# A two-layer hybrid decoder trunk: the two rstd biases of the first layer computed on VectorE instead of GpSimd

## The chip, the core and the metric

The kernel runs on one core of a Trainium2 chip. Its engines work side by side, each through its own list of instructions in order: TensorE (PE: matmuls; PEld: its weight loads), ScalarE (ACT), VectorE (DVE), GpSimd (POOL) and SyncE (SP), whose queue issues the DMAs here. An instruction waits for semaphores that instructions of other engines, or landing DMAs, raise. The metric is the device time of one execution in microseconds (us). A profile covers one execution, and its span runs from the first to the last instruction of the program.

## What is computed

Two layers work on x of 256 positions by 1024 channels in float32. Each normalises x, projects it, runs three branches of heads on parts of the projection, gates them, projects the result back and adds it to x. A last normalisation follows. The part that matters here is the normalisation of the first layer:

```python
def rms_norm(x, gain):
    xf = x.astype(jnp.float32)
    xf = xf * lax.rsqrt(jnp.mean(xf * xf, axis=-1, keepdims=True) + EPS)
    return (xf * gain.astype(jnp.float32)).astype(x.dtype)

def hybrid_layer(x, ...):
    hn = rms_norm(x, norm_gain)
    proj = jnp.einsum('bsd,de->bse', hn, w_in)
    a_q, a_k, a_v, a_g, b_x, b_g, c_q, c_k, c_v, c_g = jnp.split(proj, ...)
    # branch A: rotary positions, dilated attention
    # branch B: convolution and a gated linear recurrence
    # branch C: stick-breaking attention
    y = jnp.concatenate([y_a, y_b, y_c], axis=-1)
    return x + jnp.einsum('bse,ed->bsd', y, w_out)
```

## The kernel before

The 256 positions are two tiles of 128 partitions (t = 0 and 1), the 1024 channels eight tiles of 128 (k). A float32 product is made of three passes of matmuls over operands split in a high part and a remainder: `xh`, `xl` for the activations, `whi`, `wlo` for the weights. The passes are (whi, xh), (whi, xl), (wlo, xh), in this order (`mm3`, L202 to L207).

The weights come in chunks of 128 x 2048 (`load_chunk`, L95 to L105): for each half, SP issues a DMA of 512 KB into a buffer `st` (L100); ScalarE copies it in two pieces to `whi` (L103), and VectorE subtracts to get `wlo` (L104). There are five `st` buffers (`WST`, L32), and a buffer can be loaded again once the `wlo` pieces made from it are done. The order of the chunks is fixed: the values of branch A and C are made from the `first` loads (L136 to L165), then follow the chunks CQ and CK (queries and keys of branch C), AQ0 and AK0 (queries and keys of the first four heads of A), BX (branch B), AQ1 and further.

In the first layer the projections start from x scaled by the gain only; the factor rstd of each position is put on afterwards. `rms_stats(t)` (L186) makes it: ScalarE squares the two halves of `xres` (x as it was loaded) and sums each along the channels (L189, the sum goes to `sq`); then GpSimd makes `ss` = sq0 / 1024 + EPS (L191), and ScalarE makes `ln` = Ln(sq1 / 1024 + ss), with `ss` as the bias, and rstd = Exp(-0.5 ln) (both through the helper at L82). ScalarE then uses rstd to evict the values (`va`, L318, and `vc`, L319). VectorE uses it at L310: two diagonal matrices, which TensorE multiplies by ones (L311), so that rstd lies along a row; VectorE copies that to `rb` (L312) and scales with it the queries `qc` and keys `kc` of branch C (L324). The scores of branch C (`sb_scores`, L372 to L379) need `qc` and `kc`.

Each engine runs its list in order. TensorE's list is in the order of the code (`tc.manual_schedule`, L90, names PE alone); those of ScalarE, VectorE, GpSimd and SP come from the scheduler of the tile framework. GpSimd has little to do: it computes `log_sigmoid_lambda` (L231 to L254), a chain of some 25 instructions on tiles of 128 x 4, each waiting for the one before, whose results `c8` and `nc8` are used much later in branch B. After that chain, in its list, stand the six instructions of L191: two for the first layer, two for the second, two for the last normalisation.

On ScalarE the first layer's list around the change is: pieces of CQ (L103), the two squares of t = 0, Ln of t = 0, the two squares of t = 1 with Exp of t = 0 between them, `va` and `vc` with Ln and Exp of t = 1 between them, and then the pieces of CK, AQ0, AK0, BX, and the first half of AQ1.

Of the kernel before, what the change touches and what calls it, by code (L numbers as in the profile page):

```python
# [13 lines left out]
ALU = mybir.AluOpType  # L14
# [3 lines left out]
D = 1024  # L18
L = 2
NT = S // P  # L20
# [4 lines left out]
EPS = 1e-6  # L25
# [22 lines left out]
def trunk_kernel(ctx: ExitStack, tc: tile.TileContext, x, first_x, first, wpack, prm_d, gatew, gains, consts, rope, out):  # L48
    nc = tc.nc
    act, dve, pe, gps = nc.scalar, nc.vector, nc.tensor, nc.gpsimd  # L50
# [13 lines left out]
    def scr(w):  # L64
        return wk.tile([P, 512], F32, name="scr", tag="scr", bufs=SCR)[:, 0:w]
# [15 lines left out]
    def tab(*a, **k):  # L81
        i = dep(act.activation(*a, **k), loaded["load"])  # L82
        loaded["users"].append(i)
        return i
# [98 lines left out]
    idb = cst.tile([P, P], BF16, name="idb")  # L183
    cmb = cst.tile([P, P], BF16, name="cmb")

    def rms_stats(t):  # L186
        sq = wk.tile([P, 2], F32, name="sq", tag="sq", bufs=2)
        for i in range(2):
            act.activation(scr(512), xres[:, t, i * 512:(i + 1) * 512], AF.Square, accum_out=sq[:, i:i + 1])  # L189
        ss = wk.tile([P, 1], F32, name="ss", tag="ss", bufs=2)  # L190
        gps.tensor_scalar(ss, sq[:, 0:1], 1.0 / D, EPS, ALU.mult, ALU.add)  # L191
        ln = wk.tile([P, 1], F32, name="lnv", tag="lnv", bufs=2)
        tab(ln, sq[:, 1:2], AF.Ln, bias=ss, scale=1.0 / D)
        rstd = wk.tile([P, 1], F32, name="rstd", tag="rstd", bufs=4)
        tab(rstd, ln, AF.Exp, scale=-0.5)
        return rstd
# [10 lines left out]
            pe.matmul(ps, a(k), b(k), start=first and i == 0, stop=last and i == len(seq) - 1)  # L207

    def normed(t):
        rstd = rms_stats(t)  # L210
        xns = []
        for half in range(2):
            xn = scr(512)
            cs = slice(half * 512, half * 512 + 512)
            dve.scalar_tensor_tensor(xn, xres[:, t, cs], rstd, gn[:, cs], ALU.mult, ALU.mult)
            xns.append(xn)
        return xns
# [43 lines left out]
    for l in range(L):  # L261
# [27 lines left out]
        if l > 0:  # L289
            xn1 = normed(1)  # L290
            av_w = [weights(l, CH_AV + i, 1 - i) for i in range(2)]
            cv_w = weights(l, CH_CV, 0)
            av_ps, cv_ps = [], bank(pp, "pp")
            for t in range(NT):
                av_ps.append(bank(at, "s"))
                for i in range(2):
                    proj_a(av_ps[t], av_w[i], t, 4 * i, 4, 512, i == 0, i == 1)
                if t == 0:
                    turn(xn1, 1, xh, xl)
                proj_a(cv_ps[:, t * 256:(t + 1) * 256], cv_w, t, 0, 8, 256, True, True)  # L300
            cv_bk = [cv_ps[:, t * 256:(t + 1) * 256] for t in range(NT)]

        if l == 0:
            rstd0 = [rms_stats(t) for t in range(NT)]

        def rows_of_rstd():
            rb_ps = bank(yp, "y")
# [270 lines left out]
        for t in range(NT):  # L578
            if t == 1 and l == 0:
                next_x = [sb.tile([P, NK, S], F32R, name=n, tag=n) for n in ("xh", "xl")]  # L580
                xn0 = normed(0)
            for n2 in range(2):
                cs = slice(n2 * 512, n2 * 512 + 512)
                for ks in ((0, 1), (2, 3)):
                    out_mm(o_ps[t, n2], ow[n2], t, 1, ks, False, ks[0] == 2)
                    if (l, t, n2, ks[0]) == (0, 1, 1, 0):
                        turn(xn0, 0, *next_x)
                dve.tensor_add(xres[:, t, cs], o_ps[t, n2], xres[:, t, cs])  # L588

    for t in range(NT):  # L590
        rstd = rms_stats(t)
        for half in range(2):
            cs = slice(half * 512, half * 512 + 512)
            ot = scr(512)
            dve.tensor_mul(ot, xres[:, t, cs], gf[:, cs])
            if half == 0:
                dve.tensor_scalar(ot, ot, rstd, None, ALU.mult)
            else:
                act.activation(ot, ot, AF.Copy, scale=rstd)
            nc.sync.dma_start(out=out[t * P:(t + 1) * P, cs], in_=ot)  # L600
# [108 lines left out]
```

## Time and profile before

| | us |
|---|---|
| median of 3 runs | 257.91 |
| lowest and highest of them | 255.73, 257.99 |
| the profiled execution, whole | 258.01 |
| its span | 256.2 |
| TensorE busy | 245.9 (96% of the span) |
| VectorE busy | 190.8 (74%) |
| ScalarE busy | 163.7 (64%) |
| GpSimd busy | 9.5 (4%) |

Times of a view count from the start of the span. In rows of the timeline stand the start, the length, the engine, the line, the operation, what is written and read with sizes, how many instructions are merged, and in brackets how long the engine had been idle just before and what ended that. A row of the chain of waits has the start, the length and what ran. A row of the view of waits has the waiting instruction, what it waited for, the total, the number of waits and the longest.

### The profile page before, as it was taken

Reading aid. Unit: us, or ns where it says so; the run is one execution under the profiler, and the core shown is the slowest. Engines: PE = TensorE matmul, PEld = TensorE weight load, DVE = VectorE, ACT = ScalarE, POOL = GpSimd, SP = SyncE. Lnnn points to the kernel's source line nnn. Section 1 sums busy time; section 2 is a strip of 40 time slices with the busy share of each in tenths; the row PEclk is TensorE's granted clock in tenths of the full one; section 3 lists DMA queues with packets and bytes.
Section 4 is the critical chain, followed back from the end, with each engine's and each line's share of the span. In section 5 each row is a group of like instructions: output and inputs, shape, how many; then the busy total and the mean of one; then the engine's idle time right before and its main releaser. Section 6 shows DMA issues by size and latency. Waiting matters only on the chain.

```text
span 256.2 us, 4730 instructions
## 1 busy us (share of the span) xinstructions
PE 245.9 (96%) x1777; PEld 223.7 (87%) x1777; DVE 190.8 (74%) x427; ACT 163.7 (64%) x355; POOL 9.5 (4%) x35
## 2 busy tenths in 40 slices
PE   7999699999999999999999999999999999999990
PEld 3889599999899899978889899999999979987870
DVE  4873299999999778996594564499999856894243
ACT  3864967964594669994582765594485468993143
POOL 0037000000000000000010000000000000000000
PEclk9999979999999999999999999999999999999997
DMA  7989679862526815157448387522643742000022
GB/s 224 376 291 409 240 226 314 296 236 82 160 88 216 263 62 164 36 186 278 159 124 258 112 283 276 181 89 77 185 145 115 236 145 79 5 0 0 3 82 82
DMA packets 13126, 43.44 MB, mean 170 GB/s; under 512 B 1584, under 2 KB 2224, under 8 KB 13104
## 3 DMA queue, kind: packets, MB, share of 16 engines
q1 hardware_dynamic: 12816, 42.89, 49.6%
q8 instruction: 14, 0.23, 0.3%
q10 hardware_dynamic: 288, 0.26, 0.3%
q14 instruction: 8, 0.07, 0.1%
HBM read 42.09 MB, written 1.05 MB: 168 GB/s over the span
## 4 chain that ended last, share of the span: by engine, by line
PE 86%; DMA 4%; ACT 3%; POOL 3%; issue 1%; DVE 1%; SPq 0%; ACTq 0%
PE pp L207 63%; PE s L207 9%; DMA st<-first 4%; PE y L358 3%; PE s L426 2%; PE s L455 2%; PE s L399 1%; PE pp L481 1%; POOL ls L249 1%; POOL ls L248 1%; PE s L372 1%; PE s L223 1%; ACT scr L189 1%; ACT whi L153 1%; PE s L379 0%
## 5 line engine op out<-in xcount | busy, mean ns | idle before, releaser
L104 DVE TENSOR_TENSOR wlo<-st,whi 128x512 fp32r<-128x512 f32 x132 | 84.7, 688 | 26.3 <-ACT whi L103 25.7
L103 ACT ACTIVATE whi<-st 128x512 fp32r<-128x512 f32 x132 | 74.1, 623 | 35.8 <-PE pp L207 17.2
L207 PE MATMUL pp<-xh,whi 128*128 128x256 f32 x352 | 51.2, 287 | 2.4 <-ACT whi L103 2.4
L207 PE MATMUL pp<-xl,whi 128*128 128x256 f32 x352 | 50.2, 286 | 0.0
L207 PEld LDWEIGHTS pp<-xh,whi 128*128 128x128 f32 x352 | 46.2, 193 | 4.4 <-ACT whi L103 3.1
L207 PE MATMUL pp<-xh,wlo 128*128 128x256 f32 x352 | 49.6, 284 | 0.0
L207 PEld LDWEIGHTS pp<-xl,whi 128*128 128x128 f32 x352 | 46.2, 195 | 0.0
L207 PEld LDWEIGHTS pp<-xh,wlo 128*128 128x128 f32 x352 | 45.7, 193 | 0.0
L82 ACT ACTIVATE pr<-scr,mn 128x128 f32<-128x128 f32 (+1 forms) x32 | 14.1, 445 | 9.2 <-DVE mn L433 9.2
L189 ACT ACTIVATE scr<-xres 128x512 f32<-128x512 f32 x12 | 7.5, 626 | 13.0 <-DVE xres L588 12.9
L207 PE MATMUL pp<-whi,yh 128*128 128x512 f32 x48 | 14.1, 394 | 0.0
L207 PE MATMUL pp<-wlo,yh 128*128 128x512 f32 x48 | 13.8, 390 | 0.0
L207 PE MATMUL pp<-whi,yl 128*128 128x512 f32 x48 | 13.8, 389 | 0.0
L76 ACT ACT_TABLE_LOAD x9 | 11.5, 1283 | 1.8 <-PEq L702 1.6
L82 ACT ACTIVATE scr<-scr 128x384 f32<-128x384 f32 (+1 forms) x20 | 10.8, 540 | 0.5 <-DVE scr L324 0.3
L207 PEld LDWEIGHTS pp<-wlo,yh 128*128 128x128 f32 x48 | 9.0, 188 | 1.9
L207 PEld LDWEIGHTS pp<-whi,yl 128*128 128x128 f32 x48 | 9.0, 188 | 1.9
L207 PEld LDWEIGHTS pp<-whi,yh 128*128 128x128 f32 x48 | 8.7, 188 | 1.6
L191 POOL TENSOR_SCALAR ss<-sq 128x1 f32<-128x1 f32 x6 | 1.8, 306 | 221.3 <-ACT scr L189 220.2
L346 ACT ACTIVATE yh<-scr 128x512 fp32r<-128x512 f32 x8 | 5.1, 633 | 7.6 <-DVE scr L345 7.5
L433 DVE CUSTOM_DVE_ANT_0 scr<-s,con 128x128 f32<-128x128 f32 (+1 forms) x32 | 9.2, 354 | 0.6 <-PE s L426 0.6
L588 DVE TENSOR_TENSOR xres<-pp,xres 128x512 f32<-128x512 f32 x6 | 4.1, 690 | 7.3 <-PE pp L207 7.3
(160 smaller groups left out, 353.5 us busy)
## 6 DMA issues: line engine op xcount, KB each, us to landing
st<-w_pack SPq DMA_DIRECT2D x66, 512.0 KB, 5.0
st<-first SPq DMA_DIRECT2D x7, 512.0 KB, 5.6
xres<-x_in SPq DMA_DIRECT2D x2, 512.0 KB, 8.2
out<-scr SPq DMA_DIRECT2D x4, 256.0 KB, 2.2
gw_t<-gate_w SPq DMA_DIRECT2D x2, 256.0 KB, 6.5
gn<-gains SPq DMA_DIRECT2D x1, 512.0 KB, 6.5
gf<-gains SPq DMA_DIRECT2D x1, 512.0 KB, 6.0
st<-first ACTq DMA_DIRECT2D x2, 128.0 KB, 3.5
```

Source lines behind the costliest of these rows:

```text
L76: load = act.preload_act_table_set(name)
L82: i = dep(act.activation(*a, **k), loaded["load"])
L103: act.activation(hi[:, ws], st[:, ss], AF.Copy)
L104: dve.tensor_sub(lo[:, ws], st[:, ss], hi[:, ws].bitcast(F32))
L189: act.activation(scr(512), xres[:, t, i * 512:(i + 1) * 512], AF.Square, accum_out=sq[:, i:i + 1])
L207: pe.matmul(ps, a(k), b(k), start=first and i == 0, stop=last and i == len(seq) - 1)
L346: act.activation(yh[:, k0:k0 + n, :], dst, AF.Copy)
L358: pe.matmul(y[hr, p * 128 + o:p * 128 + 256], vt[:, s0, hs], wts[i][:, ws], start=s0 == 0, stop=s0 == 1)
L426: pe.matmul(sps[h][:, cs], qT[h0][hr, hb, t * P:(t + 1) * P], kT[h0][hr, hb, 0:(t + 1) * P], start=True, stop=True)
L433: dve.tensor_tensor_reduce(xs[:, cs], sps[h][:, cs], nmask[:, cs], -0.125, 3e38, ALU.add, ALU.min, mn[:, t:t + 1])
L455: pe.transpose(tp[:, i * P:(i + 1) * P], prob[h0 + h][:, j * P:(j + 1) * P], ident)
L588: dve.tensor_add(xres[:, t, cs], o_ps[t, n2], xres[:, t, cs])
```

## The change

`rms_stats` gets the engine of its bias instruction as an argument. The calls of the first layer hand it VectorE; the calls of the second layer (through `normed`) and of the last normalisation hand it GpSimd, as before. The operation, its operands and its result are the same.

```diff
-    def rms_stats(t):
+    def rms_stats(t, eng):
         sq = wk.tile([P, 2], F32, name="sq", tag="sq", bufs=2)
         for i in range(2):
             act.activation(scr(512), xres[:, t, i * 512:(i + 1) * 512], AF.Square, accum_out=sq[:, i:i + 1])
         ss = wk.tile([P, 1], F32, name="ss", tag="ss", bufs=2)
-        gps.tensor_scalar(ss, sq[:, 0:1], 1.0 / D, EPS, ALU.mult, ALU.add)
+        eng.tensor_scalar(ss, sq[:, 0:1], 1.0 / D, EPS, ALU.mult, ALU.add)
...
-        rstd = rms_stats(t)
+        rstd = rms_stats(t, gps)
...
-            rstd0 = [rms_stats(t) for t in range(NT)]
+            rstd0 = [rms_stats(t, dve) for t in range(NT)]
...
-        rstd = rms_stats(t)
+        rstd = rms_stats(t, gps)
```

In VectorE's list of the first layer, the place is between the last remainders of the chunk CQ and those of the chunk CK (`wlo_381`); the numbers behind names count the tiles as they are made, so `ss_306` is that of t = 0 and `ss_317` that of t = 1:

```order
 L104 TENSOR_TENSOR wlo_268<-st_269,whi_267 128x512 x2
 L104 TENSOR_TENSOR wlo_268<-st_275,whi_267 128x512 x2
+L191 TENSOR_SCALAR ss_306<-sq_301 128x1
+L191 TENSOR_SCALAR ss_317<-sq_312 128x1
 L512 CAST idb_291<-con_284 128x128
 L104 TENSOR_TENSOR wlo_381<-st_382,whi_380 128x512 x2
```

Both instructions now stand ahead of the cast of the identity `idb` and of all work on CK.

In GpSimd's list, the place is the end of the chain of `log_sigmoid_lambda`, whose last two instructions write `c8` and `nc8`:

```order
 L253 TENSOR_SCALAR c8_293<-c8_293 128x4
 L254 TENSOR_SCALAR nc8_294<-c8_293 128x4
-L191 TENSOR_SCALAR ss_306<-sq_301 128x1
-L191 TENSOR_SCALAR ss_317<-sq_312 128x1
 L191 TENSOR_SCALAR ss_1602<-sq_1597 128x1
 L191 TENSOR_SCALAR ss_1659<-sq_1654 128x1
```

They no longer stand behind that chain; the instruction that follows it now belongs to the second layer. The lists of TensorE, ScalarE and SP have the same instructions in the same order as before.

## The prediction, made before the changed kernel had run

> **What bounds the kernel now.** I read the view of waits of TensorE first, since it is busy for 96% of the span: once for the whole span, then for 36 to 250 us, where it has no row at all. Its one wait of size comes before that:
>
> ```profile
> PE pp L207 <- ACT whi L103: 2.4, 1, 2.4
> ```
>
> So the kernel goes at the speed of TensorE from 36 us on, and what can be won from outside it lies ahead of that. The timeline of TensorE shows what stands around this wait:
>
> ```profile
> 26.05 1.12 PE L207 MATMUL pp<-xl,whi 128*128 128x256 f32 x8
> 27.01 1.12 PE L207 MATMUL pp<-xh,wlo 128*128 128x256 f32 x8
> 30.54 2.35 PE L207 MATMUL pp<-xh,whi 128*128 128x256 f32 x8 [2.41 <-ACT whi L103]
> 32.70 1.91 PE L207 MATMUL pp<-xl,whi 128*128 128x256 f32 x8
> 34.40 1.35 PE L207 MATMUL pp<-xh,wlo 128*128 128x256 f32 x8
> 35.59 0.60 PE L311 MATMUL y<-scr,ones 128*128 128x128 f32 x4
> 35.95 1.20 PE L207 MATMUL pp<-xh,whi 128*128 128x256 f32 x8
> ```
>
> A pass of eight matmuls is followed by the next after 0.96 us (26.05 to 27.01); the last pass of CQ therefore ends its turn at 27.97. CK begins only at 30.54, because ScalarE had no `whi` ready, and its first three passes take 2.16, 1.70 and 1.19 us instead of 0.96. Why ScalarE is late, its own timeline and that of GpSimd say:
>
> ```profile
> 21.64 0.19 ACT L189 ACTIVATION_READ_ACCUMULATOR scr<-xres 128x1 f32 x1
> 22.25 0.19 ACT L189 ACTIVATION_READ_ACCUMULATOR scr<-xres 128x1 f32 x1
> 26.06 0.29 ACT L82 ACTIVATE lnv<-sq,ss 128x1 f32<-128x1 f32 x1 [3.62 <-POOL ss L191]
> 26.26 0.62 ACT L189 ACTIVATE scr<-xres 128x512 f32<-128x512 f32 x1
> 29.86 5.30 ACT L103 ACTIVATE whi<-st 128x512 fp32r<-128x512 f32 x10
> 43.71 0.49 ACT L383 ACTIVATE scr<-s 128x384 f32<-128x384 f32 x1 [1.23 <-PE s L379]
> ```
>
> ```profile
> 25.53 0.22 POOL L254 TENSOR_SCALAR nc<-c 128x4 f32<-128x4 f32 x1
> 25.84 0.19 POOL L191 TENSOR_SCALAR ss<-sq 128x1 f32<-128x1 f32 x1
> ```
>
> The first two rows end with the two sums of t = 0, at 21.83 and 22.44. `ss` takes 0.19 us, but stands in GpSimd's list behind a chain that ends at 25.76. ScalarE sits for 3.62 us at Ln, and everything behind it in its list is late by that, the first piece of CK (29.86) included. The chain of waits passes through the same places: GpSimd's chain, Ln, the evictions, L103, TensorE.
>
> **The change, part by part.** Removed from GpSimd: two instructions of 0.19 us. The one left behind them belongs to the second layer, so GpSimd's own time is worth nothing here. Added to VectorE: the same two. Its nearest rows, and where it stands idle:
>
> ```profile
> 16.15 0.17 DVE L251 TENSOR_SCALAR ls<-prm_t 128x4 f32<-128x4 f32 x1
> 23.25 0.23 DVE L512 CAST idb<-con 128x128 bf16<-128x128 f32 x1 [1.43 <-DMA con<-consts]
> 30.52 2.50 DVE L104 TENSOR_TENSOR wlo<-st,whi 128x512 fp32r<-128x512 f32 x4 [7.04 <-ACT whi L103]
> ```
>
> VectorE is through with CQ at 21.82 (23.25 - 1.43). The first `ss` can follow the first sum at 21.83. No TENSOR_SCALAR of 128 x 1 stands in VectorE's rows here; the bounds are the 0.17 us of four columns here and the 0.23 us of 128, and the first is the nearest: done by about 22.0, before ScalarE has the second sum, and by either bound. So Ln starts at about 22.44, not 26.06: 3.62 us earlier. Of VectorE's time the two cost nothing, since the idle 7.04 us ahead of CK cover them; without that cover they would cost 0.34 (two of 0.17).
>
> The second `ss` is a new wait in VectorE's list. It waits for the squares of t = 1, and `idb` and the remainders of CK wait behind it. Those squares need the second half of `xres`:
>
> ```profile
> L172 SPq DMA_DIRECT2D xres<-x_in x2: 424/428/433, 13.3 to 13.8; - x2
> DMA to landing us min/median/max: 7.7/8.2/8.8
> ```
>
> It lands between 21.5 (13.8 + 7.7) and 22.6 (13.8 + 8.8); I take 22.6, the later one, for the later half. The square of t = 1 starts 0.20 us after Ln in the trace (26.06 to 26.26), so at 22.64, and nothing is late. The wait ends with the first sum of t = 1 at about 23.4 (0.62 for the square and 0.19 to read out), over two microseconds before VectorE gets a piece of CK. Its price is nothing, as the same squares precede CK in ScalarE's list too.
>
> All that ScalarE does up to CK moves by 3.62: the first piece of CK to 26.24. What could hold it is the landing of the weights. The halves of CK, then of AQ0, then the first of AK0 and the second:
>
> ```profile
> L100 SPq DMA_DIRECT2D st<-w_pack x2: 517/554/592, 17.4 to 18.1; - x2
> DMA to landing us min/median/max: 8.4/8.7/9.0
> ...
> L100 SPq DMA_DIRECT2D st<-w_pack x2: 328/328/328, 19.9 to 21.1; - x2
> DMA to landing us min/median/max: 8.5/8.5/8.5
> ...
> L100 SPq DMA_DIRECT2D st<-w_pack x1: 327/327/327, 23.3 to 23.3; - x1
> DMA to landing us min/median/max: 7.9/7.9/7.9
> ...
> L100 SPq DMA_DIRECT2D st<-w_pack x1: 328/328/328, 31.8 to 31.8; - x1
> DMA to landing us min/median/max: 3.7/3.7/3.7
> ```
>
> CK lands at 25.8 and 27.1. Ten pieces take 5.30 us, 0.53 each, so the pieces of CK run from 26.24, 26.77, 27.30 and 27.83, the last done by 28.5: each landed in time. AQ0 lands at 28.4 and 29.6, within 0.2 of ScalarE's turn at 28.36 and 29.42; the first half of AK0 lands at 31.2 and makes ScalarE wait for 0.7, but VectorE comes to it at 33.7 only (37.30 - 3.62, in the rows further down). TensorE, free at 27.97, uses one piece in a quarter of a pass (0.24 us), so it wants the last at 28.7. It doesn't stop, and the 2.41 us are gone. The pass of 2.16 us was the pace of ScalarE's pieces (four of 0.53), so that goes as well. For the other two the view of windows has a reason:
>
> ```profile
> 32.70:34.40 1.70, 1.70 (x9) 1.70 (x9) 1.70 (x5) 1.70 (x4) 0.00 (x0) 0.50 0.79 222
> 36.20:39.00 2.80, 2.80 (x25) 2.80 (x25) 2.73 (x5) 0.90 (x3) 0.00 (x0) 1.00 0.80 249
> ```
>
> Each row has the stretch, its length, the busy time of the five engines, and then the granted clock: 0.50 some two microseconds behind the gap, 1.00 from 36.2. I read the halved clock as the consequence of the gap, and let it go with the gap. Then L311 starts at 27.97 + 3 x 0.96 = 30.85, and the second half of CK at 30.85 + 0.36 (35.59 to 35.95) = 31.21 instead of 35.95: **4.74 us earlier**. In parts: 27.97 to 30.54 is 2.57 us, and the three passes give back 1.20, 0.74 and 0.23.
>
> [...]
>
> What is late next? VectorE moves by 3.62 only, TensorE by 4.74, so where TensorE waits for VectorE the spare time shrinks by 1.12:
>
> ```profile
> 37.30 2.49 DVE L104 TENSOR_TENSOR wlo<-st,whi 128x512 fp32r<-128x512 f32 x4
> 39.70 0.69 DVE L324 SCALAR_TENSOR_TENSOR kc<-pp,rb 128x512 f32<-128x512 f32 x1
> 41.87 0.70 PE L372 MATMUL s<-qc,kc 64*128 64x256 f32 x4
> 45.31 0.69 DVE L104 TENSOR_TENSOR wlo<-st,whi 128x512 fp32r<-128x512 f32 x1 [0.64 <-ACT whi L103]
> 47.85 0.56 DVE L391 TENSOR_TENSOR sl<-scr,sh 128x384 fp32r<-128x384 f32 x1
> 49.65 0.23 PE L397 MATMUL s<-sh,trir 128*128 128x128 f32 x1
> ```
>
> `kc` would be done at 40.39 - 3.62 = 36.77, and TensorE wants it at 41.87 - 4.74 = 37.13: 0.36 to spare. The remainder `sl` of the first head would be done at 48.41 - 3.62 = 44.79 at worst, wanted at 44.91; as VectorE also drops its 0.64 us of idle time on the way, 0.7 to spare. Both hold, narrowly; beyond, ScalarE and VectorE wait for TensorE again (1.23 at L383), and TensorE has no wait to its end, so nothing takes the gain back. The DMAs are issued as `st` buffers come free, so they move along: the second half of AK0 is issued at about 31.8 - 3.6 = 28.2.
>
> The sum against the profiled execution: 258.01 - 4.74 = 253.27, so 253.3 us. That execution stands 0.10 above the median of 257.91.
>
> **The rivals.**
>
> VectorE becomes the bound. If one of the two narrow places doesn't hold, TensorE falls back to VectorE's shift: 258.01 - 3.62 = 254.4. For it speaks that VectorE is busy for 2.73 of the 2.80 us from 36.2 to 39.0; against it the 0.36 and 0.7 us worked out.
>
> [...]
>
> The second half of AK0 lands late, and the kernel is slower. VectorE does its remainder ahead of `kc`, in the trace 1.25 us into the four that start at 37.30 (half of 2.49), so from 34.9 on. It may land at 34.3 (its first piece takes 0.6), and TensorE notices from 34.7, with the 0.36. Issued at 28.2, it has behind its 3.7 us in an empty queue up to 9.0 us in a full one: 31.9 to 37.2. The spacing of the landings ahead (27.1, 28.4, 29.6, 31.2) puts it near 32.5. At 37.2 TensorE would stop for 2.5 us and pay 0.97 for the clock again: 258.01 - 4.74 + 3.47 = 256.7. From 38.5 on, 10.3 us after the issue, nothing is left, and beyond that the kernel is slower; no DMA of this line takes so long.
>
> Nothing changes, because Ln in truth waits for something else. Then it stays at 258.0. Against it: the sums are done at 22.44 and `ss` at 26.03, and Ln starts 0.03 after `ss`.
>
> A lower time than forecast. One run of before took 255.73, 2.18 below the median, and the trace of one execution doesn't say where that spread lies. If it lies in the stretch that the change shortens, for instance in GpSimd's chain, the changed kernel doesn't gain from it twice. If it lies elsewhere, the changed kernel may show it too: 253.3 - 2.2 = 251.1.
>
> **How the numbers follow.** The forecast, 253.3 with its own range 252.5 to 254.0, gets 0.60: two places must hold narrowly. VectorE as the bound (254.4) gets 0.14, the slow passes (254.2) 0.06, the lower time (251.1) 0.06, the late landing short of a loss (256.7) 0.05, no change (258.0) 0.05, and a loss 0.04. The range of 252.3 to 255.0 takes in the first three, 0.80, with half a microsecond for the spread of runs. About 1% (2.6 us) is what a measurement of this kernel can tell from no change, so faster begins below 255.3: 0.60 + 0.14 + 0.06 + 0.06 = 0.86. Within: 0.10. Slower: 0.04.
>
> **What would show it.** Right: Ln starts near 22.5 in ScalarE's timeline, its wait for GpSimd is gone, L103 of CK starts near 26.2, TensorE has no wait at L207, the granted clock is 1.00 from 22 to 60, L372 starts near 37.1, and the span is near 251.5. Wrong: a wait of TensorE for `kc` (L324) or `sl` (L391); a clock below 1.00 without a gap ahead; a wait of ScalarE for a landing of AK0 after 34.3; or a wait of VectorE at L191 that lasts beyond 26, which would mean that the squares of t = 1 hold up CK.

## The result, and the profile after

| | before | after |
|---|---|---|
| median of the runs, us | 257.83 (4 runs, 255.73 to 257.99) | 253.81 (4 runs, 253.48 to 254.88) |
| the profiled execution, us | 258.01 | 253.61 |
| its span, us | 256.2 | 251.8 |

The ratio of the runs is 0.9879, with a 95% interval of 0.9831 to 0.9926: the changed kernel is faster by 0.7 to 1.7%. 253.3 had been forecast, within 252.3 to 255.0.

The timeline of TensorE after the change, at the place shown in the prediction, down to the first scores of branch C:

```profile
27.36 1.12 PE L207 MATMUL pp<-xh,wlo 128*128 128x256 f32 x8
28.32 1.12 PE L207 MATMUL pp<-xh,whi 128*128 128x256 f32 x8
29.28 1.12 PE L207 MATMUL pp<-xl,whi 128*128 128x256 f32 x8
30.24 1.12 PE L207 MATMUL pp<-xh,wlo 128*128 128x256 f32 x8
31.20 0.60 PE L311 MATMUL y<-scr,ones 128*128 128x128 f32 x4
31.56 1.20 PE L207 MATMUL pp<-xh,whi 128*128 128x256 f32 x8
37.49 0.70 PE L372 MATMUL s<-qc,kc 64*128 64x256 f32 x4
```

No row has a bracket: CK begins 0.96 us after the last pass of CQ, and its three passes take 0.96 each. In the windows the granted clock, the third column from the right, is full throughout:

```profile
28.10:30.90 2.80, 2.80 (x26) 2.80 (x25) 2.80 (x7) 2.62 (x5) 0.00 (x0) 1.00 0.95 344
30.90:34.20 3.30, 3.30 (x30) 3.30 (x30) 3.27 (x9) 2.31 (x4) 0.00 (x0) 1.00 0.85 257
```

ScalarE's timeline has lost the wait for GpSimd, and has a short one for the second half of `xres` in its place:

```profile
21.75 0.19 ACT L189 ACTIVATION_READ_ACCUMULATOR scr<-xres 128x1 f32 x1
21.98 0.29 ACT L82 ACTIVATE lnv<-sq,ss 128x1 f32<-128x1 f32 x1
22.62 0.63 ACT L189 ACTIVATE scr<-xres 128x512 f32<-128x512 f32 x1 [0.35 <-DMA xres<-x_in]
26.23 4.64 ACT L103 ACTIVATE whi<-st 128x512 fp32r<-128x512 f32 x8
```

VectorE's shows the two instructions, and the two narrow places:

```profile
21.36 0.15 DVE L191 TENSOR_SCALAR ss<-sq 128x1 f32<-128x1 f32 x1
23.38 0.15 DVE L191 TENSOR_SCALAR ss<-sq 128x1 f32<-128x1 f32 x1 [1.86 <-ACT scr L189]
26.89 2.50 DVE L104 TENSOR_TENSOR wlo<-st,whi 128x512 fp32r<-128x512 f32 x4 [3.23 <-ACT whi L103]
35.84 0.68 DVE L324 SCALAR_TENSOR_TENSOR kc<-pp,rb 128x512 f32<-128x512 f32 x1
43.51 0.55 DVE L391 TENSOR_TENSOR sl<-scr,sh 128x384 fp32r<-128x384 f32 x1
```

The second `ss` holds VectorE for 1.86 us, and VectorE is idle for another 3.23 before CK, so that wait is covered.

A measure that leaves out where an execution happens to be when CQ starts is the stretch from the first pass of CQ to L372. In the first profile of before it is 41.87 - 22.21 = 19.66 us; after, with CQ at 22.56, it is 37.49 - 22.56 = 14.93. From L372 to the end of the span both have the same, 256.2 - 41.87 = 214.3 and 251.8 - 37.49 = 214.3. The whole gain lies in that stretch, and nothing is given back behind it. One run among the experiments below (only t = 1 on VectorE) took 1358.7 us, with TensorE busy for 1349.3 us of it (245.9 before the change), and its time is left out.

### The profile page after: what moved, and what is told of

Read it like the earlier page. It is cut to its first block, busy times and chain, and to the rows that moved or that the text cites. A ratio compares the mean times of both kernels' runs of the same rounds, so it can differ in the third digit from the quotient of the medians.

```text
span 251.8 us, 4728 instructions
## 1 busy us (share of the span) xinstructions
PE 244.2 (97%) x1777; PEld 223.1 (89%) x1777; DVE 190.7 (76%) x429; ACT 163.9 (65%) x355; POOL 8.3 (3%) x33
## 4 chain that ended last, share of the span: by engine, by line
PE 97%; ACT 1%; DVE 0%; issue 0%; ACTq 0%
PE pp L207 66%; PE s L207 9%; PE s L163 5%; PE y L358 3%; PE s L426 2%; PE pp L163 2%; PE s L455 2%; PE s L399 1%; PE pp L481 1%; PE y L134 1%; PE s L372 1%; PE s L223 1%; PE s L379 0%; PE s L397 0%; PE s L375 0%; ACT scr L189 0%
## 5 line engine op out<-in xcount | busy, mean ns | idle before, releaser
L207 PE MATMUL pp<-xh,whi 128*128 128x256 f32 x352 | 50.0, 285 | 0.0
L207 PE MATMUL pp<-xl,whi 128*128 128x256 f32 x352 | 49.4, 283 | 0.0
L207 PEld LDWEIGHTS pp<-xl,whi 128*128 128x128 f32 x352 | 45.4, 192 | 0.0
L446 DVE TENSOR_SCALAR pr<-pr,den 128x128 f32<-128x128 f32 (+1 forms) x32 | 8.7, 315 | 0.3
```

The costliest lines, as they stand in the source:

```text
L446: dve.tensor_scalar(pr[:, cs], pr[:, cs], den[:, t:t + 1], None, ALU.mult)
```

## The experiments

All kernels are compared with runs of the kernel before on the same chip. There that had a median of 256.96 us over 19 runs (first four experiments) and of 257.33 over 13 (the next four), both below the 257.83 of the result; the spread is the subject of the last profiles.

**GpSimd keeps both instructions, ahead of its chain.** A dependency for the order alone puts the chain's third instruction behind the second `ss`; the lists of all other engines stay.

```diff
-        gps.tensor_scalar(ss, sq[:, 0:1], 1.0 / D, EPS, ALU.mult, ALU.add)
+        bias_of.append(gps.tensor_scalar(ss, sq[:, 0:1], 1.0 / D, EPS, ALU.mult, ALU.add))
...
-        gps.tensor_mul(sv, e, d2)
+        dep(gps.tensor_mul(sv, e, d2), bias_of[1])
```

> Both bias instructions stay on GpSimd, but stand ahead of the chain of log_sigmoid_lambda in its list. Theory (the place behind the chain was the cost): Ln of t = 0 starts near 22.4 as with VectorE, TensorE has no wait at L207, the time is that of the changed kernel, 253.3 to 254.0. Rival (the gain comes from VectorE being the quicker engine for this instruction, or from GpSimd as such): the time stays near 258.

253.22 us (253.07 to 253.42), ratio 0.9859 (0.9808 to 0.9909). GpSimd's timeline:

```profile
21.55 0.19 POOL L191 TENSOR_SCALAR ss<-sq 128x1 f32<-128x1 f32 x1 [4.50 <-ACT scr L189]
23.16 0.19 POOL L191 TENSOR_SCALAR ss<-sq 128x1 f32<-128x1 f32 x1 [1.43 <-ACT rstd L82]
23.43 0.20 POOL L243 TENSOR_TENSOR ls<-ls,ls 128x4 f32<-128x4 f32 x1
```

GpSimd waits for ScalarE here and not the other way round, and the stretch from CQ to L372 is 37.20 - 22.27 = 14.93, that of the changed kernel to the hundredth. The engine didn't matter here (the first `ss` took 0.19 us on GpSimd, 0.15 on VectorE); the place behind the chain did. The time is a little below the lower end of what was expected, and its interval overlaps that of the change, so neither is shown to be the faster.

**Only t = 0 on VectorE.**

```diff
-            rstd0 = [rms_stats(t, dve) for t in range(NT)]
+            rstd0 = [rms_stats(t, (dve, gps)[t]) for t in range(NT)]
```

> Only the bias of t = 0 goes to VectorE, that of t = 1 stays on GpSimd behind the chain, which ends between 25.0 and 25.8. Theory: Ln of t = 0 starts near 22.4; Ln of t = 1, at 24.5 in the changed kernel, starts at 25.3 to 26.1, so ScalarE is 0.8 to 1.5 late at CK, of which TensorE feels 0 to 0.9: 253.6 to 254.6. Rival (the two weigh alike): about 255.8.

254.53 us (10 runs), ratio 0.9911 (0.9884 to 0.9938). Ln of t = 1 now waits for GpSimd:

```profile
25.86 0.30 ACT L82 ACTIVATE lnv<-sq,ss 128x1 f32<-128x1 f32 x1 [1.95 <-POOL ss L191]
```

TensorE has no wait by name, but the first pass of CK goes at ScalarE's pace (its ten pieces from 27.58 on take 5.31 us): it starts at 28.27 and the second at 30.16, 1.89 us for 0.96. Most of the gain is there; the rest needs both.

**Only t = 1 on VectorE.**

```diff
-            rstd0 = [rms_stats(t, dve) for t in range(NT)]
+            rstd0 = [rms_stats(t, (gps, dve)[t]) for t in range(NT)]
```

> Only the bias of t = 1 goes to VectorE, that of t = 0 stays on GpSimd behind the chain. Theory: Ln of t = 0 still starts near 26, TensorE waits 2.4 at L207, nothing is won: 257.5 to 258.3. Rival (the two weigh alike): about 255.8.

257.94 us (9 runs), ratio 1.0035 (0.9998 to 1.0072): nothing is won. The same kernel, one more execution, for its profile:

> Only the bias of t = 1 on VectorE, once more, since the profile of its first submission is of an execution in which TensorE ran some five times slower throughout. Theory: Ln of t = 0 starts near 26 behind the chain and TensorE waits about 2.4 at L207, as in the kernel before. Rival (half of the gain): Ln near 24, a gap near 1.

256.43 us. Ln of t = 0 starts at 25.32 behind the chain, earlier than the 26 expected, and TensorE waits 1.80, less than the 2.4:

```profile
29.80 2.06 PE L207 MATMUL pp<-xh,whi 128*128 128x256 f32 x8 [1.80 <-ACT whi L103]
31.70 1.12 PE L207 MATMUL pp<-xl,whi 128*128 128x256 f32 x8
```

The gap is within what the profiles of the kernel before show (1.61 to 2.41, below), so the first `ss` carries the change, and the second alone is worth nothing.

**TensorE's gap filled.** The kernel before, with 20 matmuls on `xh` and `xl` between CQ and CK, into a bank that nobody reads.

```diff
+        fill = lambda l: [pe.matmul(fb, xh[:, 0, 0:P], xl[:, 0, :], start=True, stop=True) for fb in (bank(yp, "y")[:, 0:256],) * FILL * (l == 0)]
...
-        ck_ps = proj_b(CH_CK, rows_of_rstd if l == 0 else None)
+        fill(l); ck_ps = proj_b(CH_CK, rows_of_rstd if l == 0 else None)
```

> The kernel before, with 20 more matmuls of 128x256 on loaded operands (into an unused bank) between CQ and CK, which fill TensorE's gap of 2.4 us; their result isn't used. Behind the first passes of CK the order of some VectorE and ScalarE work differs too, so the passes are read, not the total. Theory (the gap halves the clock): the second and third pass of CK take 0.96 us each and the clock stays at 1.00, while the first keeps ScalarE's pace, 2.1. [...]

256.68 us, one run. TensorE's timeline, and the windows over the three passes:

```profile
28.25 2.56 PE L417 MATMUL y<-xl,xh 128*128 128x256 f32 x20
30.65 1.89 PE L207 MATMUL pp<-xh,whi 128*128 128x256 f32 x8
32.38 1.10 PE L207 MATMUL pp<-xl,whi 128*128 128x256 f32 x8
```

```profile
30.65:32.38 1.73, 1.70 (x10) 1.13 (x9) 1.73 (x4) 1.73 (x4) 0.00 (x0) 1.00 0.01 2
32.38:33.32 0.94, 0.94 (x10) 0.94 (x9) 0.94 (x4) 0.94 (x3) 0.00 (x0) 1.00 0.31 70
33.32:34.29 0.97, 0.97 (x11) 0.97 (x10) 0.97 (x3) 0.97 (x3) 0.00 (x0) 1.00 1.02 321
```

ScalarE is as late as before (Ln at 26.00), the first pass is still slow, 1.73, but the next two take 0.94 and 0.97 at full clock. So the first pass is paced by ScalarE (ten pieces in 5.31 us), even at full clock, and the two behind it are not: with the clock up they are fast. That the clock stayed up because TensorE kept working is not shown by this one execution, since the unchanged kernel keeps its clock in about half of its runs too (below).

**The chain longer and shorter.** The series in `log_sigmoid_lambda` has 8 terms, and each costs two GpSimd instructions. With fewer terms the result is a little less exact.

```diff
-        n = 8
+        n = 16
```

In the kernel before, with 16 terms:

> The kernel before with 16 instead of 8 terms in the series of log_sigmoid_lambda: eight more pairs of GpSimd instructions of about 0.29 each with the wait between them, 4.7 us; the bias of t = 0 stands two instructions further forward, 0.6. Theory: Ln of t = 0 starts near 30, TensorE's gap grows to about 6.5, the time to about 262. Rival (the chain isn't on the path): 258.

262.24 us (261.79 to 262.62), ratio 1.0204 (1.0149 to 1.0259). Ln of t = 0 starts at 29.54; TensorE's wait, and the clock of its second pass:

```profile
34.02 2.35 PE L207 MATMUL pp<-xh,whi 128*128 128x256 f32 x8 [5.77 <-ACT whi L103]
```

```profile
36.16:37.87 1.71, 1.71 (x9) 1.71 (x9) 1.71 (x5) 1.71 (x4) 0.00 (x0) 0.50 0.81 225
```

In the changed kernel, with 16 terms:

> The changed kernel with 16 instead of 8 terms in that series. Theory: the chain is off the path, the time stays at 253.5 to 254. Rival (GpSimd's work holds something else up, by its accesses or by c8 and nc8): 255 or more.

253.82 us (253.59 to 254.25), ratio 0.9877 (0.9833 to 0.9921), and again 36.99 - 22.06 = 14.93 from CQ to L372. The chain that costs the kernel before some 5 us (262.24 against 257.33) costs this one nothing.

In the kernel before, with 4 terms:

> The kernel before with 4 instead of 8 terms (the result is a little less exact): four pairs fewer, about 2.4 us. Theory: Ln of t = 0 starts near 23.7, ScalarE begins CK near 27.5, TensorE's gap shrinks to 0.1 to 0.3, the first pass of CK keeps ScalarE's pace, the clock stays full: 254.6. If the clock falls all the same: 255.6. Rival (the chain isn't on the path): 258.

254.08 us (253.74 to 255.47), ratio 0.9896 (0.9844 to 0.9947). Ln of t = 0 starts at 23.36, TensorE's timeline has no wait, and the first pass of CK is still paced (28.13 to 29.74, 1.61 for 0.96):

```profile
28.13 1.77 PE L207 MATMUL pp<-xh,whi 128*128 128x256 f32 x8
29.74 1.11 PE L207 MATMUL pp<-xl,whi 128*128 128x256 f32 x8
```

And with 6 terms:

> The kernel before with 6 instead of 8 terms: two pairs fewer, about 1.2 us. Theory: Ln of t = 0 starts near 24.9, TensorE's gap is about 1.3. If a gap of 1.3 leaves the clock full: 255.9; if it halves it as 2.4 does: 256.8. Rival (the chain isn't on the path): 258.

255.55 us (10 runs), ratio 0.9942 (0.9914 to 0.9971), the value for a full clock, which the windows of its profile show (1.00 from 28.00 to 29.10 and from 29.20 to 33.00). Ln starts at 24.70:

```profile
29.18 2.06 PE L207 MATMUL pp<-xh,whi 128*128 128x256 f32 x8 [1.07 <-ACT whi L103]
31.08 1.12 PE L207 MATMUL pp<-xl,whi 128*128 128x256 f32 x8
```

The start of Ln, 23.36, 24.70, 26.06 (the first profile of before) and 29.54 for 4, 6, 8 and 16 terms, and the time, 254.08, 255.55, 257.33 and 262.24, go together. The length of GpSimd's chain is the cause of the stall.

**Three more profiles of the kernel before.** Nothing is changed in it.

> The kernel before, unchanged, for a further profile, as its executions spread over 255.6 to 258.5 and those of the changed one over less than half of that. Theory: the spread sits in the stretch that the change shortens, so the time from the start of CQ to L372, 19.66 us in the first profile, differs between executions by as much as the whole time, through the end of GpSimd's chain or the clock behind the gap. Rival: the spread sits elsewhere (the loads at the start, or the long stretch from L372 on), and 19.66 stays within 0.3.

> As for the look before this one: a further execution of the unchanged kernel before.

> As for the first of these looks: a further execution of the unchanged kernel before.

257.90, 256.38 and 257.77 us. Profiles 2, 3 and 4 of the kernel before (1 is the one that the prediction read), in each TensorE's wait and the pass behind it:

```profile
30.52 2.35 PE L207 MATMUL pp<-xh,whi 128*128 128x256 f32 x8 [1.93 <-ACT whi L103]
32.67 1.91 PE L207 MATMUL pp<-xl,whi 128*128 128x256 f32 x8
```

```profile
30.17 2.06 PE L207 MATMUL pp<-xh,whi 128*128 128x256 f32 x8 [1.61 <-ACT whi L103]
32.07 1.11 PE L207 MATMUL pp<-xl,whi 128*128 128x256 f32 x8
```

```profile
30.71 2.35 PE L207 MATMUL pp<-xh,whi 128*128 128x256 f32 x8 [1.89 <-ACT whi L103]
32.86 1.70 PE L207 MATMUL pp<-xl,whi 128*128 128x256 f32 x8
```

The windows of profiles 2 and 3 from 32.7 to 34.4:

```profile
32.70:34.40 1.70, 1.70 (x10) 1.70 (x10) 1.70 (x5) 1.70 (x4) 0.00 (x0) 0.50 0.78 236
```

```profile
32.70:34.40 1.70, 1.70 (x18) 1.70 (x16) 1.70 (x6) 1.70 (x5) 0.00 (x0) 1.00 0.93 260
```

| the kernel before | whole | CQ starts | Ln starts | gap | L372 | CQ to L372 | L372 to the end |
|---|---|---|---|---|---|---|---|
| profile 1 | 258.01 | 22.21 | 26.06 | 2.41 | 41.87 | 19.66 | 214.3 |
| profile 2 | 257.90 | 22.67 | 26.04 | 1.93 | 41.78 | 19.11 | 214.3 |
| profile 3 | 256.38 | 22.64 | 25.69 | 1.61 | 40.27 | 17.63 | 214.3 |
| profile 4 | 257.77 | 22.90 | 26.23 | 1.89 | 41.65 | 18.75 | 214.4 |

In these four profiles the spread lies in the stretch that the change shortens (17.63 to 19.66), and a smaller part in the start of CQ (22.21 to 22.90); behind L372 there is none. In profile 3 the gap is shorter and the clock doesn't fall, and with that it is 1.4 to 1.6 us faster than the other three. Its three passes of CK take 1.90, 0.95 and 0.96, those of profile 1 2.16, 1.70 and 1.19: the fall of the clock costs 1.24 us there, 0.26 of it in the first pass, which ScalarE paces in both.

Profile 3 is no exception. The mean granted clock of the whole execution, which is on record for each of the 32 runs of before among the experiments, parts them in two groups: 15 runs with 0.993 to 0.996 took 255.63 to 256.93 us (median 256.21), and 17 with 0.987 to 0.990 took 256.96 to 258.50 (median 257.72). A fall to one half for 3.4 us, as the profiles show it (last section), lowers the mean of 256 us by 0.007 (an estimate, 1.7 / 256), which is the distance of the two groups. So the clock falls in about half of the executions of the kernel before.

## Why the prediction was right, point by point

- Ln was to follow the second sum at once. It did: the sum ends at 21.94 and Ln starts at 21.98. The first `ss` took 0.15 us, where 0.17 was taken.
- The new wait in VectorE's list was priced at nothing. It ended at 23.38 (23.4 was worked out), 3.23 us of idle time behind it were left, and nothing that it held up was late.
- CK on ScalarE was to begin at 26.24; it began at 26.23. The wait for the second half of `xres`, 0.35, had been bounded but not counted; as everything before it was half a microsecond earlier in this execution, it cost nothing against the sum.
- The second half of AK0, on which the rival of a loss rested, was issued at 28.2 and landed after 4.3 us at 32.5, as worked out from the spacing; the rival's turning point was 34.3.
- 4.74 us were to be won at L372. Between the two profiles the stretch from CQ to L372 fell by 19.66 - 14.93 = 4.73.
- The sum was 0.34 low against the profiled execution, 253.27 against 253.61, and that is its one term that was off: it took the start of CQ from the profile of before, 22.21, and here CQ started at 22.56. That start lies between 22.06 and 22.90 in the profiles of this study. The forecast time did not hang on which execution of before had been profiled, since it was added up from CQ on: the four profiles of before, each less its stretch plus 14.93, give 253.28 to 253.95.
- VectorE didn't become the bound. `kc` was done at 36.52 and TensorE came to it at 37.49, so 0.97 were to spare where 0.36 had been worked out: 0.35 from the later CQ, the rest because VectorE came out 0.25 further forward. `sl` was done at 44.06 and its matmul started at 45.55. Of these 1.49, 0.29 are a misreading: the prediction took the row at 49.65, which is the matmul of `sh`, for that of `sl`, which started at 49.94 in the profile of before.
- That the slow passes would go with the gap was argued from the clock's column alone. For the 254.2 in which they stay no run shows a cause; in the changed kernel both take 0.96, not 1.70 and 1.19. That it was the clock, profiles 1 and 3 of before show: with a gap and a paced first pass ahead in both, the second pass takes 1.70 where the clock has fallen and 0.95 where it hasn't. That the fall comes with the gap, the mean clocks of the runs show (last section); the run with the gap filled agrees, but would not show it alone.
- One thing was taken too simply. The prediction took the halved clock as certain behind the gap. In profile 3 it didn't come, as in 15 of the 32 runs, so against such an execution of before the change wins 17.63 - 14.93 = 2.70, and against profile 1 4.73. So the 4.74 are the gain against an execution with the fallen clock and the longest gap of the four profiles, not that of an average run. The medians lie between: 257.83 - 253.81 = 4.02, or 256.96 - 253.81 = 3.15 with the 19 runs of before among the experiments.
- One part of the sum was put down to the wrong cause. The 1.20 us of the first pass of CK were taken as ScalarE's pace alone; at full clock the same pace makes 1.90 for 0.96 (profile 3), so 0.94 of it are the pace and 0.26 the clock. The total is the same, as both went.
- The rival of a lower time supposed that the spread might lie elsewhere. It lies mostly in the shortened stretch, and no run of the changed kernel was below 253.48.

The parts of the gain are thus of two kinds. The wait of 2.57 and the pace of the first pass, 0.94, follow from the place in GpSimd's list; the wait varies with the length of its chain. The clock's 0.26 and 0.97, some 1.2 together, come on top in about half of the executions.

## What to carry to other kernels

A short instruction on a nearly idle engine can hold up the whole kernel (here 0.19 us of work, and a wait of 3.62 on ScalarE for it), if it stands in that engine's list behind a long chain that nobody waits for: look for a wait on an engine that is busy for 4% of the span, and see what stands ahead of the instruction waited for. Here moving it to another engine and moving it ahead of the chain were worth the same. Where the bounding engine stops, count also what its clock does behind the gap (0.50 behind four of the seven gaps seen ahead of CK), and take more than one profile, since that part comes and goes from execution to execution.

## What the runs showed of the hardware

The clock fell to 0.50 behind gaps of TensorE of 1.89, 1.93, 2.41 and 5.77 us, and stayed at 1.00 in the windows behind gaps of 1.07, 1.61 and 1.80. Behind each the first pass was slow: 1.90 us behind the last three and 2.14 to 2.16 behind the others, where a pass without a gap takes 0.96. How long the half clock lasted is worked out from the mean clock of the windows at its edges, on the reading that it is 1.00 or 0.50 at any moment (an estimate):

| | gap | windows at the edges, mean clock | half from, to | us |
|---|---|---|---|---|
| the kernel before, profile 1 | 2.41 | 30.50 to 32.70 at 0.73, 34.40 to 35.70 at 0.80 | 31.51, 34.92 | 3.4 |
| profile 2 | 1.93 | 30.00 to 32.70 at 0.75, 34.40 to 35.40 at 0.82 | 31.35, 34.76 | 3.4 |
| profile 4 | 1.89 | 30.00 to 32.70 at 0.64, 32.70 to 34.40 at 0.57 | 30.76, 34.16 | 3.4 |
| the kernel before, 16 terms | 5.77 | 28.10 to 34.00 at 0.82, 37.87 to 39.22 at 0.68 | 31.88, 38.73 | 6.9 |

In profile 1 windows of a quarter of a microsecond agree: 1.00 in 31.25 to 31.50, 0.52 in 31.50 to 31.75, 0.66 in 34.75 to 35.00 and 1.00 in 35.00 to 35.25. At 5.77 it lasted about twice as long, and began within the gap.

How often it falls goes with the gap. With 16 terms, where the profile has a gap of 5.77, the mean clock of all four runs is 0.981 to 0.983; of the 32 runs of before (1.6 to 2.4) it is 0.990 or less in 17; with 6 terms (1.07) in one of ten, the longest; and in the 22 runs of kernels whose profile has no wait of TensorE there (the changed one, GpSimd's ahead of the chain, t = 0 only, 4 terms) it is never below 0.991. Without a fall this mean spreads by as much (0.991 to 0.998), so it tells groups of runs apart and not every single run. Fourteen of these 22 are of the kernels with t = 0 only and with 4 terms, whose profiles have a slow first pass all the same (1.89 and 1.61), so by this measure the slow pass without a gap is not enough. Whether a gap without a slow pass behind it is, was not tested.

One run stands apart: the profile of the changed kernel with 16 terms has a mean clock of 0.948, where the other three runs of that kernel have 0.992 to 0.994. TensorE has no wait in it from 15 to 60 us, and its passes of CQ and the first three of CK (22.06 to 30.70) take 0.96 us like the others. Its cause is open.

GpSimd's small instructions took more than twice as long while VectorE ran its subtractions of two operands. VectorE's timeline of profile 3 of the kernel before, and GpSimd's at the same time:

```profile
19.86 2.50 DVE L104 TENSOR_TENSOR wlo<-st,whi 128x512 fp32r<-128x512 f32 x4 [2.27 <-ACT whi L103]
```

```profile
19.70 0.22 POOL L249 TENSOR_SCALAR ls<-ls 128x4 f32<-128x4 f32 x1
20.00 0.61 POOL L248 TENSOR_TENSOR ls<-ls,ls 128x4 f32<-128x4 f32 x1
20.70 0.54 POOL L249 TENSOR_SCALAR ls<-ls 128x4 f32<-128x4 f32 x1
21.32 0.50 POOL L248 TENSOR_TENSOR ls<-ls,ls 128x4 f32<-128x4 f32 x1
21.90 0.54 POOL L249 TENSOR_SCALAR ls<-ls 128x4 f32<-128x4 f32 x1
22.52 0.20 POOL L248 TENSOR_TENSOR ls<-ls,ls 128x4 f32<-128x4 f32 x1
```

The four instructions that fall into VectorE's group take 0.50 to 0.61, those ahead of it and behind it 0.20 to 0.22. This adds some 1.3 us to the chain in this execution, and so to the stall. The trace shows the two together; what in GpSimd's instructions takes the longer time was not tested.
